# A longer order for the first operations, the values' input on two engines, the attention branch's low parts later, and differences of squares ahead of weights

## The chip, the cores and the metric

The kernel runs on one core of one Trainium2 chip. What counts is the time of one execution on the device, in microseconds (us), as the median of several runs. The engines are named as the profile names them: PE is TensorE (matmuls and transposes), DVE is VectorE, ACT is ScalarE, POOL is GpSimd, and SP issues most transfers. Each has its own queue of instructions, which it works off in order; an instruction waits at the head of its queue until what it reads is there and what it writes is free.

## What is computed

One layer of an encoder on 512 tokens of width 1024, in float32. The input is normalised, one wide projection feeds two branches, neighbourhood attention and a bidirectional Mamba-2 scan (SSD); each is projected back, weighted by a sigmoid gate and summed; then an MLP with squared ReLU follows. Both sub-layers end in a layer norm.

```python
h = layer_norm(x, ln0_g, ln0_b)
proj = u @ w_in          # q | k | v | z | x B C | dt | gates
ya = neighbourhood_attention(q, k, v, rpb) @ w_attn_br
xbc = silu(centred_dwconv(xbc, conv_w, conv_b))
dt = softplus(dt_raw + dt_bias)
y  = ssd_chunked(xs, dt, a, bm, cm) + flipped(...) + xs * d_skip
ys = rms_norm(y * silu(z)) @ w_ssd_br
mix = (sigmoid(gate_a) * ya + sigmoid(gate_s) * ys) @ w_o
h = layer_norm(DN_ALPHA * h + mix, ln1_g, ln1_b)
h = layer_norm(DN_ALPHA * h + square(relu(h @ w_ff1)) @ w_ff2, ln2_g, ln2_b)
```

## The kernel before

**Products in three.** Every large product is made of three matmuls on parts in the float32r format: a number is split into a high part (a cast by ACT) and a low part (the number less its high part, by DVE or POOL), and `mm3` (L359 to L361) adds high by high, low by high and high by low in one PSUM bank. So each slab of weights, 1 MB from memory (`ws_`), becomes `wh_` (ACT) and `wl_` (DVE or POOL) in two halves, one for the input channels 0 to 511 and one for the others, before TensorE can use it. Activations are split in the same way: `hTh` and `hTl`, `yTh` and `yTl`, `aTh` and `aTl`, `sqh` and `sql`.

**Stages.** First the head: the four tiles of 128 tokens `xt0` to `xt3` are loaded, their statistics taken (L501), the inverse root improved by one Newton step (L516 to L520, five small operations), the normalised tiles `xn` written in halves of 512 columns (L526), and transposed by TensorE (`tp_h`, L555). From these ACT makes `hTh` (L562), an engine adds the norm's offset (`hmb`, L568 or L572) and DVE makes `hTl` (L579). This is done for tokens 0 to 255 (first half) and 256 to 511 (second half). The first products are the scan's B and C channels (`wh_bc`, `ps_x`), its step sizes (`ps_dt`, then `dtT` and its transpose `tp_dt`), its x channels (`wh_x`), and its z (`ps_z`). Then come eight groups of the scan, whose results are projected (`ps_sbr`, DVE adds them up in `ysacc`, L1046); the values of the attention (`ps_v`), whose input `hBh` and `hBl` is `hTh` and `hTl` with the tokens in another order (L1125); queries and keys; sixteen heads; the attention's projection (`ps_abr`, L1304 to L1308); the merge and the output projection; the MLP. The MLP's second product (`ff2_strassen`) saves matmuls by Strassen's scheme: its operands are sums and differences of squares (`as_`, L1508) on the left and sums of weights (`w2r`, added up by transfers that accumulate) on the right.

**What sets the order.** Head, scan and their projections are operations of a planner, `Plan`: each has an engine, an estimated duration and the keys that it reads and writes; `Plan.order` simulates the engines with small random changes of the durations (`NUDGES`) and returns an order, in which `issue` emits the operations. Behind the plan the framework's scheduler orders the instructions from the order of the code and their dependencies; `behind(a, b, why)` adds one, so that `a` comes after `b`.

**The last heads.** For each head TensorE makes scores, DVE takes the maximum (L1227), ACT the exponential (L1233), DVE divides by the sum (L1237), TensorE transposes the weights (`tp_p`, two blocks per head), ACT and DVE split them (`pth`, L1252; `ptl`, L1253), and TensorE multiplies with the values (`po`, L1260). `po` has one bank (`yd`), free again when ACT has copied a part of it (`low`, L1271) and DVE has added it into `aT` (L1274). From `aT` ACT makes `aTh`, one k-slice of 128 channels per pair of heads, and DVE `aTl` (L1289); the slices of heads 14 and 15 are k = 7.

## Time and profile before

| | |
|---|---|
| median of 3 runs | 1193.47 us (1192.46 to 1193.9) |
| profiled execution | 1195.13 us, span 1193.4 us |
| PE busy | 1162.2 us (97%) |
| DVE busy | 764.2 us (64%) |
| ACT busy | 606.5 us (51%) |
| POOL busy | 547.3 us (46%) |
| first transpose | 9.88 us |
| last matmul starts | 1184.64 us |

A row of the timeline has the start in us, the duration in us, the engine, the line, the operation, what it writes and reads (partitions times elements), and how often it stands there in a row; in brackets is how long the engine was idle before it and what ended that. In the table of waits, "PE ps_v L359 <- ACT wh_v L341: 1.2, 1, 1.2" is: TensorE, at the matmuls of line 359 that write ps_v, waited 1.2 us in total, once, at most 1.2, and what came last was ACT's wh_v. A 512 wide matmul is followed by the next one after 0.227 us in the dense stretches, though its own row says 0.39, since matmuls overlap. The span is the profiled instructions from first to last; the time of the execution is longer by what lies around it.

### The profile page before, as it was taken

The page shows a single profiled execution, that of the slowest core. Times are in us where ns is not written, and L with a number is a line of the kernel's source. Part 1 is how long each engine was busy: PE and PEld are TensorE (multiplying, and loading weights), DVE is VectorE, ACT ScalarE, POOL GpSimd, SP SyncE. Part 2 cuts the span into 40 slices and gives each one's busy share as a digit, 9 for nine tenths or more (in the row PEclk, how much of TensorE's full clock was granted, in tenths as well). Part 3 has the DMA queues.
Part 4 walks back from the last instruction along what each step waited for, and adds up shares of the span by engine and source line. Part 5 has one row for each costly group of instructions (what it writes and reads, how often), then busy time and mean ns, then how long its engine had stood idle before and what let it go on. Part 6 is the DMA issues. An engine that isn't in the chain of part 4 may idle for free.

```text
span 1193.4 us, 16406 instructions
## 1 busy us (share of the span) xinstructions
PE 1162.2 (97%) x6114; PEld 988.4 (83%) x6114; DVE 764.2 (64%) x1380; ACT 606.5 (51%) x1017; POOL 547.3 (46%) x588
## 2 busy tenths in 40 slices
PE   5999999999999999999999999999999999999997
PEld 5988898989888888788888888888888888878885
DVE  7758375666756666453789975546643567398855
ACT  4586573837354654323667764342353554365510
POOL 1158977787788776403567541016046131221000
PEclk9999999999999999999999999999999999999999
DMA  7144343333333331333333213444336987778511
GB/s 231 57 146 142 89 141 106 107 106 130 106 118 106 124 124 53 106 95 87 92 86 86 59 66 106 143 145 149 95 106 180 239 201 189 183 210 221 162 55 53
DMA packets 129407, 149.19 MB, mean 125 GB/s; under 512 B 22960, under 2 KB 101808, under 8 KB 129328
## 3 DMA queue, kind: packets, MB, share of 16 engines
q1 hardware_dynamic: 115696, 112.63, 30.5%
q0 software_dynamic: 13056, 34.61, 11.9%
q8 instruction: 48, 0.79, 0.3%
q10 hardware_dynamic: 576, 0.92, 0.2%
q14 instruction: 31, 0.25, 0.1%
HBM read 145.90 MB, written 2.23 MB: 124 GB/s over the span
## 4 chain that ended last, share of the span: by engine, by line
PE 83%; DVE 6%; DMA 3%; ACT 3%; issue 3%; POOL 2%; SPq 0%; DVEq 0%; POOLq 0%; ACTq 0%
PE ps_f L361 8%; PE ps_f L359 8%; PE ps_f L360 8%; PE ps_x L361 5%; PE ps_x L359 5%; PE ps_x L360 5%; PE ps_z L359 2%; PE ps_z L360 2%; PE ps_z L361 2%; PE yd L930 2%; DMA w2r<-in_w_ff 2%; PE ps_sbr L361 2%; PE ps_sbr L359 2%; PE ps_sbr L360 2%; PE ps_g L359 2%
## 5 line engine op out<-in xcount | busy, mean ns | idle before, releaser
L737 DVE SCALAR_TENSOR_TENSOR cv<-ps_x,pc,cv 128x511 f32<-128x511 f32 (+1 forms) x128 | 95.8, 748 | 25.3 <-ACT cv L729 21.6
L360 PE MATMUL ps_f<-h1Th,wl_f 128*128 128x512 f32 (+1 forms) x288 | 104.1, 365 | 0.0
L359 PE MATMUL ps_f<-h1Th,wh_f 128*128 128x512 f32 (+1 forms) x288 | 103.7, 366 | 0.0
L361 PE MATMUL ps_f<-h1Tl,wh_f 128*128 128x512 f32 (+1 forms) x288 | 102.0, 365 | 0.0
L1494 DVE TENSOR_TENSOR wl_f<-w2r,wh_f 128x1024 fp32r<-128x1024 f32 x42 | 49.8, 1220 | 63.4 <-ACT wh_f L1493 63.4
L359 PE MATMUL ps_z<-wh_z,hTh 128*128 128x256 f32 x256 | 75.1, 293 | 0.7 <-DVE cv L737 0.7
L361 PE MATMUL ps_z<-wl_z,hTh 128*128 128x256 f32 x256 | 71.4, 279 | 0.0
L360 PE MATMUL ps_z<-wh_z,hTl 128*128 128x256 f32 x256 | 71.3, 279 | 0.0
L1488 POOL DMA_DIRECT2D w2r<-in_w_ff x30 | 36.3, 1416 | 70.7 <-DMA w2r<-in_w_ff 46.5
L359 PE MATMUL ps_f<-wh_f,sqh 128*128 128x512 f32 x168 | 65.3, 391 | 1.3 <-ACT sqh L1493 1.1
L360 PE MATMUL ps_f<-wh_f,sql 128*128 128x512 f32 x168 | 65.3, 390 | 0.2 <-DVE sql L1494 0.2
L361 PE MATMUL ps_f<-wl_f,sqh 128*128 128x512 f32 x168 | 65.3, 390 | 0.2 <-DVE wl_f L1494 0.2
L1493 ACT ACTIVATE wh_f<-w2r 128x1024 fp32r<-128x1024 f32 x42 | 42.6, 1053 | 42.1 <-DMA w2r<-in_w_ff 30.7
L1046 DVE TENSOR_TENSOR ysacc<-ps_sbr,ysacc 128x512 f32<-128x512 f32 x56 | 38.5, 689 | 39.9 <-PE ps_sbr L361 39.7
L359 PEld LDWEIGHTS ps_f<-h1Th,wh_f 128*128 128x128 f32 x288 | 53.9, 188 | 9.0 <-ACT rl L1588 0.3
L360 PEld LDWEIGHTS ps_f<-h1Th,wl_f 128*128 128x128 f32 x288 | 53.9, 188 | 8.8
L342 DVE TENSOR_TENSOR wl_f<-ws_f,wh_f 128x1024 fp32r<-128x1024 f32 x36 | 47.2, 1347 | 20.6 <-ACT wh_f L341 20.5
L361 PEld LDWEIGHTS ps_f<-h1Tl,wh_f 128*128 128x128 f32 x288 | 52.8, 188 | 8.7
L1339 POOL TENSOR_TENSOR gt<-gt,ysacc 128x512 f32<-128x512 f32 x8 | 13.2, 1656 | 100.6 <-ACT gt L1064 92.5
L359 PE MATMUL ps_x<-hTh,wh_bc 128*128 128x512 f32 (+1 forms) x144 | 56.9, 395 | 1.6 <-ACT wh_bc L464 1.6
L359 PE MATMUL ps_sbr<-yTh,wh_sbr 128*128 128x512 f32 x128 | 55.6, 435 | 1.2 <-DVE ysacc L1046 0.6
L360 PE MATMUL ps_x<-hTh,wl_bc 128*128 128x512 f32 (+1 forms) x144 | 53.6, 372 | 1.9 <-POOL wl_bc L467 1.9
(340 smaller groups left out, 3769.1 us busy)
## 6 DMA issues: line engine op xcount, KB each, us to landing
ws_f<-in_w_ff SPq DMA_DIRECT2D x20, 1024.0 KB
w2r<-in_w_ff POOLq DMA_DIRECT2D x18, 1024.0 KB, 7.6
bc<-acs_d SPq DMA_DIRECT2D x32, 512.0 KB
w2r<-in_w_ff POOLq DMA_DIRECT2D x30, 512.0 KB, 9.1
ws_bc<-in_w_in SPq DMA_DIRECT2D x16, 512.0 KB
ws_x<-in_w_in SPq DMA_DIRECT2D x8, 1024.0 KB
ws_z<-in_w_in SPq DMA_DIRECT2D x8, 1024.0 KB
ws_g<-in_w_in SPq DMA_DIRECT2D x8, 1024.0 KB
```

The source lines that it names most:

```text
L342: (eng[i] if isinstance(eng, tuple) else eng).tensor_tensor(out=lo[:, k], in0=st[:, k], in1=hi[:, k].bitcast(F32), op=ALU.subtract)
L359: nc.tensor.matmul(o, lh, rh, start=start, stop=False)
L360: nc.tensor.matmul(o, ll, rh, start=False, stop=False)
L361: return nc.tensor.matmul(o, lh, rl, start=False, stop=stop)
L737: op("DVE", 0.75, lambda j=j, o=o, n=n: nc.vector.scalar_tensor_tensor(out=acc()[:, o], in0=ps()[:, n], scalar=tap(j), in1=acc()[:, o], op ...
L930: nc.tensor.matmul(yd()[:, c % 2, h * HD : (h + 1) * HD], bc()[:, 1, h, :], xtok()[:, c, h * HD : (h + 1) * HD], start=True, stop=True)
L1046: op("DVE", 0.69, lambda d=d, ps=ps: nc.vector.tensor_tensor(out=ysacc[:, d, :], in0=ps(), in1=ysacc[:, d, :], op=ALU.add), r=[(ps.name, 0 ...
L1339: nc.gpsimd.tensor_tensor(out=g1, in0=g1, in1=ysacc[:, d, :], op=ALU.mult)
L1488: nc.gpsimd.dma_start(t, rows(i, n, c, k), accum_op=ALU.add)
L1493: nc.scalar.activation(hi[:, k], x, AF.Copy)
L1494: nc.vector.tensor_tensor(out=lo[:, k], in0=x, in1=hi[:, k].bitcast(F32), op=ALU.subtract)
```

## The change

It has four parts.

1. `HEAD` is a list of the first operations of the plan with the engine that each is to run on (S, D, A, P, T for SP, DVE, ACT, POOL, TensorE); `issue` emits these first, in this order, and then the rest in the order of the planner as before. `ON` takes the engine from the list for the halves of the low weights, `xn`, `hmb` and `wl_dt`. Where one token tile is normalised by itself, two of the Newton step's operations become one, and the operation for an offset that only ACT needs is left out when DVE does both halves.
2. Of the sixteen copies into `hBh` and `hBl`, those of k = 0 to 3 go to ACT, the others stay on DVE. An unused tile, `yT_pad`, is put in front of `yTh`, which moves `yTh` and what lies behind it in the pool's memory.
3. `aTl` for k = 2 to 5 is made behind the last block of the last head's weights. For the first two output blocks of the attention's projection, the high products for k = 0 to 5 are made first, the low ones behind the last head, then k = 6 and 7.
4. Where the left operand of a Strassen product is a difference, the low part of what is split next comes behind the difference.

The first rows of ACT show the head. Before, from the first slab's high part on:

```order
L464 ACTIVATE wh_bc_175<-ws_bc_121 128x1024
L562 ACTIVATE hTh<-tp_h_0_0_157,pc 128x256 x2
L464 ACTIVATE wh_bc_175<-ws_bc_121 128x1024
L568 ACTIVATE hmb_0_192<-hTh,nb_98 128x256
L562 ACTIVATE hTh<-tp_h_0_3_169,pc 128x256
L568 ACTIVATE hmb_6_197<-hTh,nb_98 128x256
L562 ACTIVATE hTh<-tp_h_0_2_166,pc 128x256
```

and with the change, from the first normalised half on:

```order
L572 ACTIVATE xn_147<-xt_113,ln_rs 128x512
L504 ACTIVATE wh_bc_156<-ws_bc_119 128x1024 x2
L606 ACTIVATE hTh<-tp_h_0_0_159,pc 128x256
L613 ACTIVATE hmb_0_186<-hTh,nb_98 128x256
L606 ACTIVATE hTh<-tp_h_0_1_174,pc 128x256
L606 ACTIVATE hTh<-tp_h_0_2_163,pc 128x256
L606 ACTIVATE hTh<-tp_h_0_0_159,pc 128x256
L613 ACTIVATE hmb_2_196<-hTh,nb_98 128x256
L606 ACTIVATE hTh<-tp_h_0_2_163,pc 128x256
L606 ACTIVATE hTh<-tp_h_0_1_174,pc 128x256
```

Both high halves of the slab `wh_bc` stand ahead of the first cast of `hTh`, and an `xn` half ahead of them; the orders of SP and POOL are the same as before in this place.

DVE at the last two heads (`sc` is the softmax of a head, `ptl_0` and `ptl_1` the low parts of the two blocks of its weights). Before, from the sums of head 14 on:

```order
L1235 RECIPROCAL sums_6802<-sums_6802 128x4
L1289 TENSOR_TENSOR aTl_kh<-aT,aTh 128x512 x2
L1289 TENSOR_TENSOR aTl_klz<-aT,aTh 128x512
L1237 TENSOR_SCALAR sc_6800<-sc_6800,sums_6802 128x256 x4
L1289 TENSOR_TENSOR aTl_klz<-aT,aTh 128x512
L1274 TENSOR_TENSOR aT<-po_6598,low_6609 64x8x16 x3
L1274 TENSOR_TENSOR aT<-po_6598,low_6609 64x8x8 x2
L1253 TENSOR_TENSOR ptl_1_6672<-tp_p_1_6666,pth_1_6671 128x512
```

and with the change, from head 15's division on:

```order
L1289 TENSOR_SCALAR sc_6875<-sc_6875,sums_6877 128x256 x4
L1305 TENSOR_TENSOR ptl_0_6831<-tp_p_0_6825,pth_0_6830 128x512
L1327 TENSOR_TENSOR aT<-po_6673,low_6684 64x8x16 x3
L1327 TENSOR_TENSOR aT<-po_6673,low_6684 64x8x8 x2
L1305 TENSOR_TENSOR ptl_1_6840<-tp_p_1_6834,pth_1_6839 128x512
L1342 TENSOR_TENSOR aTl_qs<-aT,aTh 128x512
L1305 TENSOR_TENSOR ptl_0_6908<-tp_p_0_6902,pth_0_6907 128x512
L1327 TENSOR_TENSOR aT<-po_6843,low_6854 64x8x16 x3
L1327 TENSOR_TENSOR aT<-po_6843,low_6854 64x8x8 x2
L1305 TENSOR_TENSOR ptl_1_6917<-tp_p_1_6911,pth_1_6916 128x512
L1342 TENSOR_TENSOR aTl_kh<-aT,aTh 128x512 x2
L1342 TENSOR_TENSOR aTl_klz<-aT,aTh 128x512 x2
```

The four rows of `aTl_kh` and `aTl_klz` stood around head 14's division and now stand behind the last block of head 15.

DVE in the MLP's second product, at the seventh Strassen product's first block (`as_7_0` is the difference, `wl_f_0_7_0` the low weights, `sql` the low squares). Before:

```order
L1494 TENSOR_TENSOR sql_8198<-as_5_1_9361,sqh_8197 128x512
L1494 TENSOR_TENSOR wl_f_0_7_0_9480<-w2r_7_0_9475,wh_f_0_7_0_9479 128x1024 x2
L1508 TENSOR_TENSOR as_7_0_9468<-r_1_8200 128x512 x2
L1494 TENSOR_TENSOR sql_8196<-as_7_0_9468,sqh_8195 128x512 x2
L1508 TENSOR_TENSOR as_7_1_9509<-r_1_8200 128x512 x2
```

and with the change:

```order
L1564 TENSOR_TENSOR sql_8196<-as_5_1_9359,sqh_8195 128x512
L1581 TENSOR_TENSOR as_7_0_9466<-r_1_8198 128x512 x2
L1564 TENSOR_TENSOR wl_f_0_7_0_9478<-w2r_7_0_9473,wh_f_0_7_0_9477 128x1024 x2
L1564 TENSOR_TENSOR sql_8194<-as_7_0_9466,sqh_8193 128x512 x2
L1581 TENSOR_TENSOR as_7_1_9507<-r_1_8198 128x512 x2
```

The difference and the low weights have changed places. The diff, with the list cut:

```diff
-XN_ENG = (("DVE", "DVE"),) * 4
+HEAD = """
+S:xt0.0 S:xt1.0 P:xt2.0 S:pc.0 S:ident.0 S:ws_bc0.1 S:ws_bc0.0 S:xt3.0 S:xt2.0 S:ws_x0.0
+S:ws_dt.0 S:r64.0 S:cst.0 S:msk.0 S:dsk.0 D:st.0.0 D:st.0.1 D:st.1.1 D:mv.0 D:st.1.0
+A:vh.0 D:mv.1 D:nv.1 A:vh.1 D:rs.1 D:xn1.1 A:xn1.0 D:nv.0 D:rs.0 D:xn0.0 A:wh_bc0.0
...
+""".split()
+ON = {x[2:]: x[0] for x in HEAD}
...
         return max(end)
 
     def issue(self):
-        for i in self.order(NUDGES):
+        order = self.order(NUDGES)
+        named = {}
+        for o in self.ops:
+            named.setdefault(".".join(map(str, o["w"][0])), []).append(o["i"])
+        head = [named[x[2:]].pop(0) for x in HEAD]
+        done = set(head)
+        for i in head + [i for i in order if i not in done]:
             self.ops[i]["fn"]()
 
 
...
-        def newton(pr=pr, vh=vh, nv=nv, y=y):
+        def newton(pr=pr, vh=vh, nv=nv, y=y, ts=ts):
             v_.reciprocal(y, vh)
-            v_.tensor_tensor(out=vh, in0=y, in1=y, op=ALU.mult)
-            v_.tensor_tensor(out=vh, in0=vh, in1=nv, op=ALU.mult)
+            if len(ts) == 1:
+                v_.scalar_tensor_tensor(out=vh, in0=y, scalar=y, in1=nv, op0=ALU.mult, op1=ALU.mult)
+            else:
+                v_.tensor_tensor(out=vh, in0=y, in1=y, op=ALU.mult)
+                v_.tensor_tensor(out=vh, in0=vh, in1=nv, op=ALU.mult)
             v_.scalar_tensor_tensor(out=y, in0=vh, scalar=1.5, in1=y, op0=ALU.add, op1=ALU.mult)
-            v_.scalar_tensor_tensor(out=rs[:, pr, 1], in0=mv[:, pr, 0], scalar=-1.0, in1=y,
-                                    op0=ALU.mult, op1=ALU.mult)
+            if any(ON[f"xn{t}.{j}"] == "A" for t in ts for j in range(2)):
+                v_.scalar_tensor_tensor(out=rs[:, pr, 1], in0=mv[:, pr, 0], scalar=-1.0, in1=y,
+                                        op0=ALU.mult, op1=ALU.mult)
...
             op("ACT", 0.5, lambda c=c: nc.scalar.activation(yz()[:, c, :], yz()[:, c, :], AF.Copy,
                                                             scale=rt["y"]()[:, c : c + 1]),
                r=[(rt["y"].name, 0), (yz.name, c)], w=[(yz.name, c)])
-        yTh = local(f"yTh{g}", "yTh", [P, 2, S], F32R)
+        def make():
+
+            if g == 0:
+                sbp.tile([P, 1728], F32, name="yT_pad")
+            return sbp.tile([P, 2, S], F32R, tag="yTh", bufs=1, name=f"yTh{g}")
+
+        yTh = Plan.Tile(plan, f"yTh{g}", "yTh", make)
         yTl = local(f"yTl{g}", "yTl", [P, 2, S], F32R)
         for i in range(2):
             tpy = bank(f"tp_y{g}_{i}", "tr", [P, NT, P])
...
     blk = "p (r b j) -> p b r j"
     for k in range(KD):
         for src, dst in ((hTh, hBh), (hTl, hBl)):
-            nc.vector.tensor_copy(dst[:, k, :].rearrange("p (b r j) -> p b r j", r=8, b=4),
-                                  src[:, k, :].bitcast(F32).rearrange(blk, r=8, b=4))
+            d4 = dst[:, k, :].rearrange("p (b r j) -> p b r j", r=8, b=4)
+            s4 = src[:, k, :].bitcast(F32).rearrange(blk, r=8, b=4)
+            if k < 4:
+                nc.scalar.activation(d4, s4, AF.Copy)
+            else:
+                nc.vector.tensor_copy(d4, s4)
     for s in range(2):
         pss = [psx.tile([P, 512], F32, tag=tag, bufs=BANKS[tag], name=f"ps_v{s}_{b}")
                for b, tag in enumerate(("so", "tr", "so", "tr"))]
...
                 pth = atp.tile([P, 2, 2, P], F32R, tag="pth", bufs=3, name=f"pth{h}_{b2}")
                 ptl = atp.tile([P, 2, 2, P], F32R, tag="ptl", bufs=3, name=f"ptl{h}_{b2}")
                 nc.scalar.activation(pth, tp, AF.Copy)
-                nc.vector.tensor_tensor(out=ptl, in0=tp, in1=pth.bitcast(F32), op=ALU.subtract)
+                spread = nc.vector.tensor_tensor(out=ptl, in0=tp, in1=pth.bitcast(F32),
+                                                 op=ALU.subtract)
                 pts.append((pth, ptl))
             po = psx.tile([P, 4, P], F32, tag="yd", bufs=BANKS["yd"], name=f"po{h}")
 
...
         t = atp.tile([P, n, S], F32R, tag=tag, name=f"aTl_{tag}")
         aTl.extend(t[:, i] for i in range(n))
     for k in range(KD):
-        nc.vector.tensor_tensor(out=aTl[k], in0=aT[:, k], in1=aTh[:, k].bitcast(F32),
-                                op=ALU.subtract)
+        low = nc.vector.tensor_tensor(out=aTl[k], in0=aT[:, k], in1=aTh[:, k].bitcast(F32),
+                                      op=ALU.subtract)
+        if 2 <= k < 6:
+            behind(low, spread, "the last head's weights")
 
 
     ya = app.tile([P, KD, S], F32, tag="aT", name="ya")
...
         wa = weights([(w_attn_br, 0, d2 * 256, 256)], KD, 256, f"abr{d2}",
                      nc.vector if d2 else nc.gpsimd,
                      after=(ins.ins, ins.ins) if d2 == 1 else None)
+        tag = ("so", "mm")[d2 % 2]
+        pss = [psx.tile([P, S], F32, tag=tag, bufs=BANKS[tag], name=f"ps_abr{2 * d2 + j}")
+               for j in range(2)]
+
+        def steps(j, ks, parts):
+            ins = []
+            for k in ks:
+                w = [t[:, k, j * P : (j + 1) * P] for t in wa]
+                for p, (u, v) in enumerate(((w[0], aTh[:, k, :]), (w[1], aTh[:, k, :]), (w[0], aTl[k]))):
+                    if p in parts:
+                        ins.append(nc.tensor.matmul(pss[j], u, v, start=k + p == 0,
+                                                    stop=k == KD - 1 and p == 2))
+            return ins
+
+        if d2:
+            for j in range(2):
+                steps(j, range(KD), (0, 1, 2))
+        else:
+
+            for j in range(2):
+                steps(j, range(6), (0, 1))
+            for j in range(2):
+                behind(steps(j, range(6), (2,))[0], last, "the last head")
+            for j in range(2):
+                steps(j, range(6, KD), (0, 1, 2))
         for j in range(2):
-            d = 2 * d2 + j
-            tag = ("so", "mm")[d2 % 2]
-            ps = psx.tile([P, S], F32, tag=tag, bufs=BANKS[tag], name=f"ps_abr{d}")
-            for k in range(KD):
-                w = [t[:, k, j * P : (j + 1) * P] for t in wa]
-                first = nc.tensor.matmul(ps, w[0], aTh[:, k, :], start=k == 0, stop=False)
-                if (d, k) in ((0, 6), (1, 0)):
-                    behind(first, last, "the last head")
-                nc.tensor.matmul(ps, w[1], aTh[:, k, :], start=False, stop=False)
-                nc.tensor.matmul(ps, w[0], aTl[k], start=False, stop=k == KD - 1)
-            nc.scalar.activation(ya[:, d, :], ps, AF.Copy)
+            nc.scalar.activation(ya[:, 2 * d2 + j, :], pss[j], AF.Copy)
     at.__exit__(None, None, None)
     vpool.__exit__(None, None, None)
 
...
 
 
         np_ = len(r2)
-        begun, made, fetched = set(), [0], [0]
+        begun, made, fetched, first = set(), [0], [0], []
 
         def rows(i, n, c, k=slice(0, 4)):
             r0 = q0 * D + (i * np_ + c) * 512
...
         def split(hi, lo, src):
             for x, k in zip(src, halves):
                 nc.scalar.activation(hi[:, k], x, AF.Copy)
-                nc.vector.tensor_tensor(out=lo[:, k], in0=x, in1=hi[:, k].bitcast(F32),
-                                        op=ALU.subtract)
+                low = nc.vector.tensor_tensor(out=lo[:, k], in0=x, in1=hi[:, k].bitcast(F32),
+                                              op=ALU.subtract)
+                if first:
+                    behind(low, first[-1], "the difference of squares first")
+            first.clear()
             return hi, lo
 
         def left(name, c, x, y=None):
...
             if y is not None:
                 t = ffp.tile([P, 4, 256], F32, tag="asum", bufs=1, name=f"as_{h}_{name}_{c}")
                 for i, k in enumerate(halves):
-                    nc.vector.tensor_tensor(out=t[:, k], in0=src[i], in1=part(*y, k), op=ALU.subtract)
+                    diff = nc.vector.tensor_tensor(out=t[:, k], in0=src[i], in1=part(*y, k),
+                                                   op=ALU.subtract)
                 src = [t[:, k] for k in halves]
             pair = pairs[made[0] % len(pairs)]
             made[0] += 1
-            return split(*pair, src)
+            both = split(*pair, src)
+            if y is not None:
+                first.append(diff)
+            return both
 
         def right(name, c, x):
             return split(*parts(f"f2_{h}_{name}_{c}", [P, 4, 512]), x)
```

71 lines of the change are left out of this document (48 added, 23 removed).

## The prediction

> **What bounds the kernel now.** I read the page's busy times first, then the table of waits of TensorE, then the timeline of each place named there.
>
> ```profile
> PE 1162.2 (97%) x6114; PEld 988.4 (83%) x6114; DVE 764.2 (64%) x1380; ACT 606.5 (51%) x1017; POOL 547.3 (46%) x588
> PE tp_h L555 <- DVE xn L526: 9.9, 1, 9.9
> PE po L1260 <- DVE aT L1274: 2.0, 2, 1.4
> PE ps_x L360 <- POOL wl_bc L467: 1.9, 1, 1.9
> PE ps_x L359 <- ACT wh_bc L464: 1.6, 1, 1.6
> PE ps_v L359 <- ACT wh_v L341: 1.2, 1, 1.2
> PE ps_f L359 <- ACT sqh L1493: 1.1, 1, 1.1
> ```
>
> TensorE is busy for 97% of the 1193.4 us. The change takes away no matmul, so it can only shorten the 31 us in which TensorE is idle, and the time in which it runs slowly. Of those 31 us, 9.9 lie ahead of the first transpose. The next five rows, 7.8 us, are the four places that the change touches. An idle engine elsewhere is no gain. Of what stands in a queue only what TensorE waits for counts, and time won there stays won only if every later wait of TensorE moves with it.
>
> **1. The head.** These are the rows of TensorE and of the engines that feed it, in the first 36 us.
>
> ```profile
> 10.15 1.06 ACT L464 ACTIVATE wh_bc<-ws_bc 128x1024 fp32r<-128x1024 f32 x1 [2.33 <-DMA ws_bc<-in_w_in]
> 11.24 1.23 DVE L467 TENSOR_TENSOR wl_bc<-ws_bc,wh_bc 128x1024 fp32r<-128x1024 f32 x1
> 14.08 1.05 ACT L464 ACTIVATE wh_bc<-ws_bc 128x1024 fp32r<-128x1024 f32 x1
> 14.67 0.68 DVE L501 BATCH_NORM_STATS2 ln_st<-xt 128x6 f32<-128x512 f32 x1
> 15.22 2.35 POOL L467 TENSOR_TENSOR wl_bc<-ws_bc,wh_bc 128x1024 fp32r<-128x1024 f32 x1 [10.50 <-ACT wh_bc L464]
> 17.62 0.58 PE L360 MATMUL ps_x<-hTh,wl_bc 128*128 128x256 f32 x1 [1.86 <-POOL wl_bc L467]
> 22.22 0.41 PE L359 MATMUL ps_x<-hTh,wh_bc 128*128 128x256 f32 x1
> 22.44 0.40 PE L360 MATMUL ps_x<-hTh,wl_bc 128*128 128x256 f32 x1
> 22.65 0.30 PE L361 MATMUL ps_x<-hTl,wh_bc 128*128 128x256 f32 x1
> 22.79 0.28 PE L359 MATMUL ps_x<-hTh,wh_bc 128*128 128x256 f32 x1
> 35.42 0.28 PE L361 MATMUL ps_dt<-hTl,wh_dt 128*64 128x256 f32 x1
> 35.74 0.59 ACT L629 ACTIVATE dtT<-ps_dt 64x512 f32<-64x512 f32 x1 [2.81 <-PE ps_dt L361]
> 51.10 0.28 PE L359 MATMUL ps_z<-wh_z,hTh 128*128 128x256 f32 x1
> ```
>
> TensorE works in one piece from 17.62, when GpSimd ends the second low half of the first slab. GpSimd began that only at 15.22, because ScalarE made the high half behind two casts of hTh, at 14.08. After the change ScalarE makes both high halves back to back, from 10.15 to 10.15 + 2 x 1.05 = 12.25, and GpSimd is done at 12.25 + 2.35 = 14.6. VectorE is then the later one: the low half at 11.24 to 12.47, three statistics at 0.64 to 0.68 each, now ahead of the first hTl (14.4), and that hTl of 0.48: 14.9. So the piece begins at 14.9 in place of 17.62: 2.7 us.
>
> TensorE needs one k-slice per three to nine matmuls of 0.21 us each at the low pitch; ScalarE (a cast of hTh and, for half of them, one of hmb) and VectorE some 1.0 us per slice, so neither starves it. The 19 pitches from 17.62 to 22.65 take 5.03 us, where 19 at 0.213 (two of them lie between 22.22 and 22.65) take 4.05: 1.0 us went in small waits. With the second products of each slice filled in between I count 0.7 of it as won. From 21 us the new order gives ScalarE 9 us of work in one piece, ending near 30.2; the last hTl follows at 30.8 and the last ps_dt near 31.5, by TensorE's own work 35.70 - 2.7 - 0.7 - 0.3 = 32.0 (three x matmuls of 0.113 now come behind it). TensorE still bounds. Cover: if ScalarE's piece were 1 us longer, it would cost 0.5.
>
> The pitch halves at 22.65, 5.03 us after the start of the piece. I let it halve 5 us after the new start, near 19.9. If it stays at 22.65, a matmul that would have taken 0.113 takes 0.213 for those 2.75 us, and 1.3 us of the gain are lost. Sum of the head: **-3.4 us**, to the first ps_z (51.10, then 47.7), from -1.5 (clock late, half of the small waits back) to -4.4 (all of them gone).
>
> [...]
>
> **2. The values' input.**
>
> ```profile
> 495.34 2.00 ACT L341 ACTIVATE wh_v<-ws_v 128x1024 fp32r<-128x1024 f32 x2
> 506.18 0.39 PE L361 MATMUL ps_sbr<-yTl,wh_sbr 128*128 128x512 f32 x1
> 506.61 0.69 DVE L1046 TENSOR_TENSOR ysacc<-ps_sbr,ysacc 128x512 f32<-128x512 f32 x1 [0.67 <-PE ps_sbr L361]
> 506.66 2.01 ACT L341 ACTIVATE wh_v<-ws_v 128x1024 fp32r<-128x1024 f32 x2 [9.31 <-issue]
> 507.22 0.42 DVE L1125 CAST hBh<-hTh 128x512 fp32r<-128x512 f32 x1
> 507.78 1.17 PE L359 MATMUL ps_v<-wh_v,hBh 128*128 128x512 f32 x4 [1.21 <-ACT wh_v L341]
> ```
>
> The wait is put down to wh_v, but that had been done since 495.34 + 2.00 = 497.34; TensorE really waits for the first hBh, which stands behind the last ysacc, itself waiting for the last ps_sbr. The pitch is 0.227, so 507.78 - 506.18 - 0.23 = 1.37 us are lost. Eight copies move to ScalarE, which was idle for 9.31 us here: at 0.6 each (its 64x512 op at 718.59 below takes 0.59) they end near 502, and the unused tile ahead of yTh keeps them from waiting for yTh's memory. What they delay on ScalarE, the second wh_v, begins at 506.66 anyway. VectorE's eight end 2.7 us sooner. **-1.3 us**; from 0 (the copies wait for the last ps_sbr after all) to -1.5.
>
> **3. The branch's low parts.**
>
> ```profile
> 701.16 1.68 DVE L1289 TENSOR_TENSOR aTl_kh<-aT,aTh 128x512 fp32r<-128x512 f32 x2
> 713.52 0.36 PE L1260 MATMUL po<-pth,vhl 128*128 128x256 f32 x1 [0.65 <-DVE aT L1274]
> 715.89 0.94 DVE L1274 TENSOR_TENSOR aT<-po,low 64x128 f32<-64x128 f32 x5 [0.52 <-ACT low L1271]
> 716.98 0.36 PE L1260 MATMUL po<-pth,vhl 128*128 128x256 f32 x1 [1.35 <-DVE aT L1274]
> 718.59 0.59 ACT L1271 ACTIVATE low<-po 64x512 f32<-64x512 f32 x1 [2.11 <-PE po L1261]
> 723.27 3.21 DVE L342 TENSOR_TENSOR wl_abr<-ws_abr,wh_abr 128x1024 fp32r<-128x1024 f32 x2 [0.17 <-ACT wh_abr L341]
> ```
>
> Beyond the normal pitch, po of heads 14 and 15 start 0.8 and 1.6 us late, together 2.4: each waits for VectorE to empty the one yd bank. VectorE loses four low parts (1.68 for two of them) ahead of the last softmax and does them behind ptl15_1, so head 15's softmax runs some 2.8 us sooner; nine matmuls of the branch (2.0 us) stand ahead of po15, which covers low14 (0.6) and the adds (0.94). Both stalls should go. But six more branch matmuls (1.4 us) now precede po15, so po15 ends only 2.4 - 1.4 = 1.0 us sooner, and the chain behind it (low, the sigmoid's table, gt, aTh7, wh_abr1, wl_abr1) moves by 1.0 while TensorE wants wl_abr1 2.4 us sooner. Before, its first half was ready at 723.27 + 3.21 / 2 = 724.9, and TensorE came for it near 725.5, 0.6 later; so 2.4 - 1.0 - 0.6 = 0.8 is late again. **-1.6 us**; from -0.8 (the aTl and aTh7 chain late too) to -2.4.
>
> **4. Differences of squares.**
>
> ```profile
> 1044.10 1.06 ACT L1493 ACTIVATE wh_f<-w2r 128x1024 fp32r<-128x1024 f32 x1 [5.05 <-DMA w2r<-in_w_ff]
> 1046.29 0.39 PE L361 MATMUL ps_f<-h1Tl,wh_f 128*128 128x512 f32 x1
> 1046.33 1.29 DVE L1508 TENSOR_TENSOR as<-r 128x512 f32<-128x512 f32 x2
> 1047.05 1.29 ACT L1493 ACTIVATE sqh<-as 128x512 fp32r<-128x512 f32 x2 [1.90 <-DVE as L1508]
> 1047.73 0.50 PE L359 MATMUL ps_f<-wh_f,sqh 128*128 128x512 f32 x1 [1.06 <-ACT sqh L1493]
> 1048.46 0.50 PE L360 MATMUL ps_f<-wh_f,sql 128*128 128x512 f32 x1 [0.23 <-DVE sql L1494]
> ```
>
> The differences need nothing that is still on its way, yet stand behind a weight half that waits for a transfer. Ahead of it they are done long before; ScalarE casts sqh right behind wh_f, 1045.16 to 1046.45, and VectorE's first sql, now behind the weight half that ScalarE released at 1045.16, ends near 1047.1. TensorE's stall of 1047.73 - 1046.29 - 0.23 = 1.21 goes, and that for sql (0.50) shrinks a little. **-1.3 us**; from 0 (w2r lands that much later) to -1.9.
>
> **Sum.** -3.4 - 1.3 - 1.6 - 1.3 = -7.6. The profiled execution took 1195.13 us, 1.7 around its span; it lies 1.7 above the median of 1193.47. I predict a span of about 1185.8 and a median of **1185.9 us**, on its own 1183.5 to 1188.5.
>
> **Rivals.**
> A. *The head gives half.* ScalarE gets the xn, hTh, hmb and weight casts in one piece, and VectorE can be held up by GpSimd:
>
> ```profile
> 20.92 2.39 POOL L467 TENSOR_TENSOR wl_x<-ws_x,wh_x 128x1024 fp32r<-128x1024 f32 x1 [3.35 <-ACT wh_x L464]
> 22.10 1.24 DVE L511 TENSOR_SCALAR ln_v<-ln_mv 128x2 f32<-128x2 f32 x1
> ```
>
> A two-element op took 1.24 us until GpSimd's slab half ended at 23.31. In the new order that slab half lies near 28.2 to 30.6, beside the last hmb and hTl; two such blocks, or x tiles that land after VectorE reaches their statistics (14.67 is when they were read, not when they landed), cost some 2.4: 1188.3. Against it: GpSimd's first half ends at 14.6 in the new order, before the first hTl.
> B. *The last two places hand theirs on*: wl_abr1 late by all it can be and w2r pacing TensorE: -0.8 and 0 in place of -1.6 and -1.3: 1188.0.
> C. *Slower: the clock stays low.* If the piece at 14.9 is broken often enough that the pitch stays at 0.21 through the second transposes, each us after 19.9 costs half of one. It outweighs the whole sum from 19.9 + 15.2 = 35.1 on; up to the first ps_z, near 47.7, it costs 13.9: 1199.8. For it: the transposes from 9.9 on did not bring the short pitch, which came 13 us later. Against it: the new queue holds 45 matmuls, 9.6 us at the low clock, ahead of the next transpose, and small waits of up to 0.6 us did not prevent it before. [...]
> D. *No change*: the w2r stream, not TensorE, sets the last stage, and what came before is waited away at 1044. For it, the 5.05 us that ScalarE waited for w2r; against it, the stream's transfers start when TensorE's results free their buffers, so they move too. Only the tail would count: about 1192.
>
> **How the numbers follow.** Forecast 0.56, A 0.16, B 0.11, C 0.05, D 0.07; 0.05 for more than forecast (all stalls gone, 1182). The range takes the forecast's own, A, B and the better case down to 1181.8 and up to 1190.5, leaving out C and most of D. Within 0.2% means within 2.4 us, which is what a measurement here can tell from no change: faster 0.56 + 0.16 + 0.11 + 0.05 = 0.88, same 0.07, slower 0.05.
>
> **What would show it.** Right: the matmul that waited at 17.62 near 15, the pitch halved near 20, dtT near 32, ps_z from 47.7; ps_v right behind ps_sbr; no wait of po for aT and a new one, under 1 us, of ps_abr for wl_abr; no wait of ps_f for sqh. Wrong: dtT later than 34, hB copies on ScalarE beginning only after the last ps_sbr, a wait for wl_abr over 1.6, or a shift at 900 us that is gone at 1060.

## The result and the profile after

The changed kernel takes 1186.38 us (median of 6 runs, 1185.48 to 1187.55), the kernel before 1193.93 us beside it (6 runs). The ratio is 0.9936, with a 95% interval from 0.9924 to 0.9949: 7.5 us faster, where 7.6 had been predicted (1185.9 us). The profiled execution took 1186.48 us, its span is 1184.7 us.

The page's busy row and four rows of TensorE's table of waits, for the changed kernel:

```profile
PE 1158.4 (98%) x6114; PEld 988.1 (83%) x6114; DVE 757.0 (64%) x1361; ACT 614.7 (52%) x1033; POOL 546.6 (46%) x588
...
PE tp_h L599 <- DVE xn L575: 10.2, 1, 10.2
PE ps_x L401 <- DVE hTl L621: 1.8, 1, 1.8
...
PE ps_abr L1363 <- DVE wl_abr L382: 0.9, 1, 0.9
...
PE ps_f L400 <- DVE sql L1564: 0.3, 1, 0.3
```

The rows of before for po, ps_v and ps_f behind sqh are gone, the two for ps_x have become one, and ps_abr is new. TensorE has as many matmuls as before. Its busy time is 3.8 us lower and the span 8.7, so more than half of the gain is idle time that went.

The four places in the changed kernel's timeline. First the head:

```profile
9.96 2.01 ACT L504 ACTIVATE wh_bc<-ws_bc 128x1024 fp32r<-128x1024 f32 x2 [0.62 <-DMA ws_bc<-in_w_in]
10.17 3.27 PE L599 MATMUL tp_h<-cst,xn 128*128 128x128 f32 x16 [10.17 <-DVE xn L575]
12.06 2.44 POOL L508 TENSOR_TENSOR wl_bc<-ws_bc,wh_bc 128x1024 fp32r<-128x1024 f32 x1 [7.48 <-ACT wh_bc L504]
12.20 1.87 DVE L542 BATCH_NORM_STATS2 ln_st<-xt 128x6 f32<-128x512 f32 x3
13.49 1.47 ACT L606 ACTIVATE hTh<-tp_h,pc 128x256 fp32r<-128x256 f32 x3 [0.52 <-PE tp_h L599]
14.99 0.48 DVE L621 SCALAR_TENSOR_TENSOR hTl<-tp_h,pc,hmb 128x256 fp32r<-128x256 f32 x1 [0.93 <-ACT hTh L606]
15.53 0.39 PE L401 MATMUL ps_x<-hTl,wh_bc 128*128 128x256 f32 x1 [1.85 <-DVE hTl L621]
31.86 0.59 ACT L671 ACTIVATE dtT<-ps_dt 64x512 f32<-64x512 f32 x1 [1.38 <-PE ps_dt L401]
47.34 0.28 PE L399 MATMUL ps_z<-wh_z,hTh 128*128 128x256 f32 x1
```

ScalarE makes both high halves in one go, GpSimd ends its low half at 14.50, and the dense work begins at 15.53 in place of 17.62. The first ps_z comes at 47.34, 3.76 us earlier. Then the values and the branch:

```profile
494.05 0.61 ACT L1176 ACTIVATE hBh<-hTh 128x512 fp32r<-128x512 f32 x1
503.00 0.39 PE L401 MATMUL ps_sbr<-yTl,wh_sbr 128*128 128x512 f32 x1
503.22 1.07 PE L399 MATMUL ps_v<-wh_v,hBh 128*128 128x512 f32 x4
707.02 0.37 PE L1313 MATMUL po<-pth,vhl 128*128 128x256 f32 x1
710.73 0.28 PE L1313 MATMUL po<-pth,vhl 128*128 128x256 f32 x1
712.09 0.59 ACT L1324 ACTIVATE low<-po 64x512 f32<-64x512 f32 x1 [2.40 <-PE po L1314]
714.76 3.00 POOL L1409 TENSOR_TENSOR gt<-gt,ysacc 128x512 f32<-128x512 f32 x2 [17.02 <-ACT gt L1112]
716.76 3.21 DVE L382 TENSOR_TENSOR wl_abr<-ws_abr,wh_abr 128x1024 fp32r<-128x1024 f32 x2 [0.16 <-ACT wh_abr L381]
718.89 0.50 PE L1363 MATMUL ps_abr<-aTh,wl_abr 128*128 128x512 f32 x1 [0.89 <-DVE wl_abr L382]
```

ps_v stands one pitch (0.22 us) behind the last ps_sbr, since ScalarE had begun its copies 9 us earlier. Both last output products come without a wait (no bracket), and the weights' low half is now late by 0.89 us. Last, the squares:

```profile
1036.89 1.06 ACT L1563 ACTIVATE wh_f<-w2r 128x1024 fp32r<-128x1024 f32 x1 [5.01 <-DMA w2r<-in_w_ff]
1037.86 1.14 ACT L1563 ACTIVATE sqh<-as 128x512 fp32r<-128x512 f32 x2
1039.18 0.39 PE L399 MATMUL ps_f<-wh_f,sqh 128*128 128x512 f32 x1
1039.87 0.50 PE L400 MATMUL ps_f<-wh_f,sql 128*128 128x512 f32 x1 [0.30 <-DVE sql L1564]
```

sqh follows wh_f directly, where ScalarE had stood idle for 1.90 us, and TensorE no longer waits for it.

### The profile page after: what moved, and what is told of

Its sections match the earlier page's. It is cut to its first block, busy times and chain, and to the rows that moved or that the text cites. A ratio compares the mean times of both kernels' runs of the same rounds, so it can differ in the third digit from the quotient of the medians.

```text
span 1184.7 us, 16407 instructions
## 1 busy us (share of the span) xinstructions
PE 1158.4 (98%) x6114; PEld 988.1 (83%) x6114; DVE 757.0 (64%) x1361; ACT 614.7 (52%) x1033; POOL 546.6 (46%) x588
## 4 chain that ended last, share of the span: by engine, by line
PE 90%; DVE 3%; DMA 3%; issue 1%; ACT 1%; POOL 1%; DVEq 0%; SPq 0%; POOLq 0%; ACTq 0%
PE ps_f L399 8%; PE ps_f L401 8%; PE ps_f L400 8%; PE ps_x L401 5%; PE ps_x L399 5%; PE ps_x L400 5%; PE ps_abr L1363 3%; PE ps_g L399 2%; PE ps_g L401 2%; PE ps_g L400 2%; PE ps_z L399 2%; PE ps_sbr L399 2%; PE ps_z L400 2%; PE ps_z L401 2%; PE ps_sbr L401 2%; PE yd L972 2%
## 5 line engine op out<-in xcount | busy, mean ns | idle before, releaser
L401 PE MATMUL ps_x<-hTl,wh_bc 128*128 128x512 f32 (+1 forms) x144 | 53.6, 372 | 1.8 <-DVE hTl L621 1.8
```

Of the source, the lines that this page charges most:

```text
L401: return nc.tensor.matmul(o, lh, rl, start=False, stop=stop)
```

## The experiments

Since each edit of the change moves TensorE at one place, the traces can be laid over each other: the n-th matmul of one against the n-th of the other. The step at a place is by how much that difference changes from just ahead of it to just behind it. It compares two single executions, so whatever only one of them met at that place stands in it too. The four parts were run one at a time first.

**Part 1 alone** (`HEAD`, `ON` and what reads them, put into the kernel before).

```diff
+HEAD = """
+S:xt0.0 S:xt1.0 P:xt2.0 S:pc.0 ...
+""".split()
+        for i in head + [i for i in order if i not in done]:
```

> Part 1 of the change alone, the rest as before. Theory (four separate stalls, each worth what its own place gives, no part needs another): tp_dt starts near 32.8 in place of 36.66, first ps_z near 47.3 in place of 51.10, and the shift stays: ps_v 3.2 us sooner than before, the end 3.2 to 3.6 us sooner; time 1190.3 to 1190.8 where before is 1193.9. Rival (the last stage is paced by the w2r transfers): the shift is there at 700 us but not at 1060 us, time within 1.5 us of before. Rival (the head is worth little and the others more): tp_dt moves by under 2 us.

**Part 2 alone.**

```diff
+            if g == 0:
+                sbp.tile([P, 1728], F32, name="yT_pad")
...
+            if k < 4:
+                nc.scalar.activation(d4, s4, AF.Copy)
+            else:
+                nc.vector.tensor_copy(d4, s4)
```

> Part 2 alone: eight copies on ScalarE and the unused tile. Theory: nothing moves ahead of 500 us; the wait of ps_v (1.21 us) is gone, everything behind is 1.4 to 1.5 us sooner, time 1192.4. Rival (the copies wait for the memory of yTh, or the eight copies hold up ScalarE's next weights): the wait of ps_v remains in part, time within 0.7 us of before.

**Part 3 alone.**

```diff
+        if 2 <= k < 6:
+            behind(low, spread, "the last head's weights")
...
+            for j in range(2):
+                steps(j, range(6), (0, 1))
+            for j in range(2):
+                behind(steps(j, range(6), (2,))[0], last, "the last head")
```

> Part 3 alone: low parts late and the branch's products reordered. Theory: both waits of po for aT are gone (2.4 us), a wait of 0.8 to 0.9 us of ps_abr for wl_abr is new; the matmuls behind 730 us are 1.6 to 2.0 us sooner, time 1191.9 to 1192.3. Rival (the new wait eats it all): shift under 0.8 us.

**Part 4 alone.**

```diff
+                if first:
+                    behind(low, first[-1], "the difference of squares first")
...
+            if y is not None:
+                first.append(diff)
```

> Part 4 alone: the difference of squares ahead of the low weights. Theory (the wait comes from VectorE's order, not from the transfer): the wait of ps_f for sqh (1.06 us) is gone; with the smaller waits around it 1.3 to 1.9 us from 1060 us on, time 1192.0 to 1192.6. Rival (part 4 only pays when TensorE comes 6.7 us sooner, as with the whole change): under 0.7 us.

The four, each timed beside the kernel before (1194.7 us, 33 runs), and TensorE's steps against the profile of before, in us. The last column is a second profile of the changed kernel (`after_again`, below).

| | part 1 | part 2 | part 3 | part 4 | all | all, again |
|---|---|---|---|---|---|---|
| median, us | 1191.97 | 1193.74 | 1191.77 | 1193.16 | 1186.38 | 1187.18 |
| ratio to before | 0.9978 | 0.9996 | 0.9978 | 0.9989 | 0.9936 | 0.9931 |
| 95% interval | 0.9969 to 0.9987 | 0.9987 to 1.0005 | 0.9966 to 0.9989 | 0.9979 to 1.0 | 0.9924 to 0.9949 | 0.9917 to 0.9945 |
| step, start to first tp_dt | -3.61 | -0.37 | -0.36 | -0.27 | -3.88 | -3.72 |
| step at the first ps_v | 0.00 | -1.46 | 0.00 | 0.00 | -1.47 | -1.47 |
| step over the last heads and ps_abr | +0.05 | +0.04 | -1.96 | +0.01 | -2.00 | -1.93 |
| step at the squares | -1.80 | -1.90 | -1.85 | -2.97 | -1.93 | -2.99 |

The second and third rows of steps are clean: each part acts at its own place, whether the others are there or not, and with its full size. The first row needs a correction: parts 2, 3 and 4 leave the head as it was, and yet it ends 0.27 to 0.37 us earlier in them, so the profile of before was late there by about 0.3, and part 1 is worth some 3.3 us at this place. By the ratios the parts are worth 2.6, 0.5, 2.6 and 1.3 us, together 7.0 of the 7.6 that the whole ratio gives, so they add up within the intervals.

Against what had been expected: parts 2 and 3 did in their traces what their theories say. Part 2's time does not show it, since its interval reaches from 1.6 us faster to 0.6 slower. Part 1 missed: its first ps_v came 2.76 us sooner than before, not 3.2, because 0.7 of the gain at the first ps_z was lost on the way, and its time fell by 2.6 us, not by 3.1 to 3.6. Part 4's time is at the lower end of its theory, but its step at the squares has to be read with the next paragraph.

The fourth row is not clean: the kernels *without* part 4 gained 1.8 to 1.9 us at the squares too. That much of the stall belonged to the one execution that was profiled before. ScalarE's cast wh_f and TensorE's product behind it, in the timeline of part 1 alone, whose squares are as before:

```profile
1039.68 1.06 ACT L1535 ACTIVATE wh_f<-w2r 128x1024 fp32r<-128x1024 f32 x1 [4.94 <-DMA w2r<-in_w_ff]
1042.63 1.29 ACT L1535 ACTIVATE sqh<-as 128x512 fp32r<-128x512 f32 x2 [1.89 <-DVE as L1550]
1043.32 0.49 PE L399 MATMUL ps_f<-wh_f,sqh 128*128 128x512 f32 x1
1044.04 0.50 PE L400 MATMUL ps_f<-wh_f,sql 128*128 128x512 f32 x1 [0.23 <-DVE sql L1536]
```

Here the transfer of w2r let wh_f begin 3.6 us ahead of TensorE's product (1043.32 - 1039.68), and sqh came just in time, although the differences still stand behind a weight half. In the profile of before, w2r came so late that only 2.4 us lay between wh_f (1044.10) and the moment TensorE was ready (1046.29 + 0.23), and sqh was 1.21 late. Its late w2r had also stopped TensorE once before, 26 us ahead of that:

```profile
1020.86 1.06 ACT L1493 ACTIVATE wh_f<-w2r 128x1024 fp32r<-128x1024 f32 x1 [6.18 <-DMA w2r<-in_w_ff]
1021.98 0.50 PE L359 MATMUL ps_f<-wh_f,sqh 128*128 128x512 f32 x1 [0.21 <-ACT wh_f L1493]
```

This product waits for the cast of w2r itself, not for a difference of squares. With two longer pitches behind it the place cost 0.6 us, and in no other profile, with part 4 or without, does it cost anything.

**The changed kernel once more.**

> The changed kernel once more, for a second profile of it beside the variants. Its time should be 1186 to 1187 again. Theory (the place of the squares differs from profile to profile by when the transfer of the second layer's weights lands, 6.4 to 8.7 us after ScalarE asks for it): TensorE's place behind the squares' first column differs from the first profile of the changed kernel by 0.5 us or more against its place ahead of it, most likely 0.7 to 1.1 us earlier. Rival (each kernel has its own stall there): the same step to within 0.2 us.

Measured: 1187.18 us (5 runs, 1184.88 to 1187.37), and a step at the squares 1.06 us larger than in the first profile, as the theory said. The same rows in this second profile:

```profile
1037.81 1.06 ACT L1563 ACTIVATE wh_f<-w2r 128x1024 fp32r<-128x1024 f32 x1 [4.62 <-DMA w2r<-in_w_ff]
1038.77 1.14 ACT L1563 ACTIVATE sqh<-as 128x512 fp32r<-128x512 f32 x2
1041.09 0.39 PE L399 MATMUL ps_f<-wh_f,sqh 128*128 128x512 f32 x1
1041.32 0.39 PE L400 MATMUL ps_f<-wh_f,sql 128*128 128x512 f32 x1
```

wh_f stands 3.28 us ahead of TensorE (in the first profile 1039.18 - 1036.89 = 2.29), and nothing waits. The pitches of over 0.3 us at this place, where 0.227 is normal, cost TensorE in all, without part 4: 2.9 (before, with the 0.6 at 1022), 1.2, 1.0 and 1.1 us (parts 1, 2, 3 alone); with part 4: 0.9 (first profile of the changed kernel), and between 0.0 and 0.6 in its second profile, part 4 alone and the variants below, in six of these nine nothing. So part 4 is worth about 1.1 us where w2r is early and 1.3 (2.26 less 0.94) where it is late. This second profile also has a wait that no part touches, of yo for t, 1.3 us, at 357.6 us: single profiles wander by such amounts.

**Without the unused tile.**

```diff
-            if g == 0:
-                sbp.tile([P, 1728], F32, name="yT_pad")
```

> The changed kernel without the tile yT_pad, so that the eight values' copies of ScalarE land again on addresses that the last attention products still read. Theory (the tile is what lets the copies start at 494 us in the changed kernel): the first copy hBh now waits for the last ps_sbr, near 503 us, the eight copies end near 508 us, and ps_v waits at least 1 us behind ps_sbr again; TensorE's place behind the branch's start is 1 to 5 us later than in the changed kernel, time 1187.5 to 1191. Rival (VectorE's four copies moved to ScalarE are the whole of it, the address is free long before): ps_v still follows ps_sbr at once, time as the changed kernel's, about 1186.4.

Measured: 1185.68 us (0.9926, 0.9912 to 0.994), no worse than with it. In its timeline the address does to seven copies what it was said to do, and not to the first:

```profile
493.26 0.62 ACT L1174 ACTIVATE hBh<-hTh 128x512 fp32r<-128x512 f32 x1
502.63 0.63 ACT L1174 ACTIVATE hBl<-hTl 128x512 fp32r<-128x512 f32 x1 [8.75 <-PE ps_sbr L401]
...
502.21 0.39 PE L401 MATMUL ps_sbr<-yTl,wh_sbr 128*128 128x512 f32 x1
502.43 1.07 PE L399 MATMUL ps_v<-wh_v,hBh 128*128 128x512 f32 x4
503.34 0.47 PE L400 MATMUL ps_v<-wh_v,hBl 128*128 128x512 f32 x1
```

Seven of ScalarE's eight copies wait 8.75 us for the last ps_sbr. But the first does not, and it is all that ps_v needs to begin: four products on hBh take 0.91 us, by when the first hBl is there (502.63 + 0.63 = 503.26 against 503.34), and nothing behind it waits. The theory was right on seven copies and wrong on the first, near 503 us by it and at 493.26 in the trace, which is the one that TensorE waits for: the tile is worth nothing that shows. What part 2 wins it wins by the second engine, by which the first copy no longer stands behind the last ysacc.

**The low parts early again**, with the new order of the products kept.

```diff
-        if 2 <= k < 6:
-            behind(low, spread, "the last head's weights")
```

> The changed kernel without the call that moves the branch's low parts behind others: the low parts 2 to 5 stand again where the kernel before had them, ahead of the last head's softmax work on VectorE, with the new order of the gate products kept. Theory (the low parts stand in front of the last head's work, and this is where the branch's stall came from): the wait of head 14's output product, 0.7 to 0.9 us, comes back, VectorE's division for head 15 is 1 to 2 us later than in the changed kernel, time 1187.0 to 1188.4. Rival (the order of the products alone did the work): no wait of 0.5 us or more at the last two heads' output products and the time of the changed kernel, about 1186.4.

Measured: 1188.03 us (0.9946, 0.9932 to 0.9959), in the range of the theory. TensorE's two waits of this place:

```profile
712.54 0.36 PE L1313 MATMUL po<-pth,vhl 128*128 128x256 f32 x1 [1.35 <-DVE aT L1327]
720.97 0.50 PE L1361 MATMUL ps_abr<-aTh,wl_abr 128*128 128x512 f32 x1 [0.88 <-DVE wl_abr L382]
```

The wait of the last head's product is back with the 1.35 us that it had before (head 14's, which I had named, is not), the wait for wl_abr stays, and the step over the place is 2.07 us worse than in the changed kernel, which is all of part 3. The order of the products alone is worth nothing; without the dependency of the low parts nothing of part 3 is left. The dependency with the old order of the products was not run.

**The last gates early.**

```diff
-                nc.scalar.activation(pth, tp, AF.Copy)
+                cast = nc.scalar.activation(pth, tp, AF.Copy)
...
-    gates.append([merge_gates(1, 0, ("cb", "mm")), merge_gates(1, 1, ("mm", "cb"), last)])
+    gates.append([merge_gates(1, 0, ("cb", "mm")), merge_gates(1, 1, ("mm", "cb"), cast)])
```

> The changed kernel with the last gates' sigmoid, and the table load ahead of it, put on ScalarE before the low part of the last head rather than behind it. ScalarE stands idle for 2.40 us there in the changed kernel, and table load and two sigmoids take 2.55 us. Theory (the chain low part, table load, sigmoids, aTh, wh_abr, wl_abr sets the first gate product, which waited 0.89 us): low part at most 0.2 us later, the weights' cast about 1 us or more earlier, the wait of ps_abr for wl_abr gone, time 0.7 to 1.0 us under the changed kernel's, about 1185.5. Rival (another operand, the last head's aT, sets that start as well): the wait keeps its length under another name, time about 1186.4.

Measured: 1186.54 us (0.9936, 0.9924 to 0.9948): the rival's time, and a wait of the old length under another name, though for aTl_klz and not for the last head's aT. The table load (1.28 us, from 711.98) went into ScalarE's idle time as intended, and yet:

```profile
714.03 3.04 POOL L1409 TENSOR_TENSOR gt<-gt,ysacc 128x512 f32<-128x512 f32 x2 [14.03 <-ACT gt L1112]
...
712.94 1.29 DVE L1342 TENSOR_TENSOR aTl_kh<-aT,aTh 128x512 fp32r<-128x512 f32 x2
714.15 3.48 DVE L1342 TENSOR_TENSOR aTl_klz<-aT,aTh 128x512 fp32r<-128x512 f32 x2
720.29 2.36 DVE L382 TENSOR_TENSOR wl_abr<-ws_abr,wh_abr 128x1024 fp32r<-128x1024 f32 x2 [0.26 <-ACT wh_abr L381]
...
717.68 0.73 PE L1363 MATMUL ps_abr<-aTl_klz,wh_abr 128*128 128x512 f32 x2 [0.96 <-DVE aTl_klz L1342]
```

The gates released GpSimd's products 3.0 us earlier (714.03, less the 2.26 us by which this whole profile is later, against 714.76), so these now run beside two other low parts of VectorE, which took 3.48 us where the two of the same form just ahead took 1.29. The weights' low part, no longer beside GpSimd, took 2.36 where it takes 3.21 in the changed kernel. So there was a third theory: what TensorE waits for at this place is GpSimd's work beside VectorE's.

**GpSimd's products late.**

```diff
+            lows[name] = (eng[i] if isinstance(eng, tuple) else eng).tensor_tensor(
...
-            nc.gpsimd.tensor_tensor(out=g1, in0=g1, in1=ysacc[:, d, :], op=ALU.mult)
+            g = nc.gpsimd.tensor_tensor(out=g1, in0=g1, in1=ysacc[:, d, :], op=ALU.mult)
+            if d2 == 1:
+                behind(g, lows["abr1"], "the next weights' low part")
```

> The changed kernel with GpSimd's two products of the second gates (gt times ysacc, 3.0 us in all) put behind the low part of the branch's second weights on VectorE. In the changed kernel they run from 714.8 to 717.8 us, beside that low part. Theory (VectorE's two halves of wl_abr take 3.21 us rather than 2.36 us because GpSimd works at the same time, and TensorE's wait of 0.89 us for wl_abr is that): the pair takes 2.3 to 2.5 us, the wait falls under 0.2 us, time 0.7 to 0.9 us under the changed kernel's. Rival (the halves wait for ScalarE's wh_abr, GpSimd does not matter): pair 3.0 us or more or the wait 0.7 us or more, time the changed kernel's.

Measured: 1184.44 us (0.9918, 0.9904 to 0.9933), 2.7 us under the changed kernel of the same job (1187.18), though the two intervals overlap. Of that the trace gives this place 0.84 us; the rest is other places and runs.

```profile
716.20 2.36 DVE L384 TENSOR_TENSOR wl_abr<-ws_abr,wh_abr 128x1024 fp32r<-128x1024 f32 x2 [0.25 <-ACT wh_abr L383]
718.64 3.38 POOL L1411 TENSOR_TENSOR gt<-gt,ysacc 128x512 f32<-128x512 f32 x2 [21.45 <-DVE wl_abr L384]
```

The pair takes 2.36 us, GpSimd begins when it is done, and ps_abr's wait has left the table of waits. That is the theory, in each of its numbers but the time, which fell by more.

**Early gates and late products together.**

```diff
+    gates.append([merge_gates(1, 0, ("cb", "mm")), merge_gates(1, 1, ("mm", "cb"), cast)])
...
+            if d2 == 1:
+                behind(g, lows["abr1"], "the next weights' low part")
```

> The early gates together with GpSimd's late products. With the early gates alone VectorE's low parts of the last heads took 3.48 us for two rather than 1.29 us, beside GpSimd's products, and the wait of 0.89 us only changed its name. Theory (GpSimd beside VectorE is what ate the early gates): the two low parts take 1.3 us again, ScalarE's last aTh is 0.5 us or more earlier than in the changed kernel against TensorE's place, no wait over 0.2 us at ps_abr, time 0.7 to 1.0 us under the changed kernel's, that is as with the late products alone. Rival (the early gates delay the last head's low part on ScalarE as well): a wait of 0.5 us or more stays at ps_abr.

Measured: 1186.04 us, but with runs from 1183.69 to 1188.58 (0.9931, 0.9913 to 0.9949), so the time tells nothing. The trace does: the low parts take 1.29 us for two again, ScalarE's last aTh comes 0.9 us earlier, nothing waits at ps_abr, and the step over the place is 1.18 us under the changed kernel's, 0.33 more than with the late products alone. GpSimd beside VectorE was what ate the early gates.

**Another head order.**

```diff
-...T:tp_h0_0_1.0 A:hTh.0.0 T:tp_h0_0_3.0 D:st.3.1 T:tp_h0_0_2.0 P:wl_bc0.1
-S:ws_bc1.1 A:hmb0_0.0 T:tp_h0_0_1.1 D:st.3.0 A:hTh.2.0 D:st.2.1 A:hTh.5.0 A:hTh.1.0
+...T:tp_h0_0_1.0 A:hTh.0.0 A:hTh.1.0 T:tp_h0_0_3.0 D:st.3.1 T:tp_h0_0_2.0 P:wl_bc0.1
+S:ws_bc1.1 A:hmb0_0.0 T:tp_h0_0_1.1 D:hmb0_1.0 D:hTl.1.0 D:hTl.0.0 A:hTh.2.0 A:hTh.3.0 D:st.3.0
...
```

> The changed kernel with another order of its first operations: the second transposed block's high part right behind the first's, and both low parts ahead of the later statistics. Theory (the first dense product waits 1.85 us for a low part that VectorE could make 1 us earlier): dense work starts near 14.4 us rather than 15.5, and the head's end, the transposes of dt, comes 0.3 to 1.3 us earlier than 32.78 us, time 1185.1 to 1186.1. Rival (the later blocks' supply sets the head's end: the last low part was ready 0.8 us before TensorE took it, and the two casts of weights come when they come): the early start is lost again in waits for hTl or x's statistics between 16 and 31 us, dt's transposes within 0.3 us of 32.78, time about 1186.4.

Measured: 1185.6 us (0.9934, 0.992 to 0.9947). Both theories get a part.

```profile
12.88 1.74 DVE L616 TENSOR_SCALAR hmb<-hTh,pc 128x256 f32<-128x256 f32 x1
15.66 0.39 PE L401 MATMUL ps_x<-hTl,wh_bc 128*128 128x256 f32 x1 [1.31 <-DVE hTl L621]
18.90 0.33 PE L400 MATMUL ps_dt<-hTh,wl_dt 128*64 128x256 f32 x1 [0.41 <-DVE wl_dt L585]
32.37 0.46 PE L676 MATMUL tp_dt<-cst,dtT 64*128 64x64 f32 x4
```

The start did not move (15.66): an offset of VectorE that takes 0.35 us alone took 1.74 us beside GpSimd's half of the slab, which ended at 14.46. This order did not get past that; no run moved the half slab to show that it is the cause here. dt's transposes come 0.40 us earlier all the same, which is less than the 0.7 us by which they differ among the eight profiles with the head order of the change (last section). The first ps_dt came at 18.21 for 19.39, since the clock stayed full there (1.00 between 16 and 20 us, for 0.58 and 0.57; last section); 0.8 of these 1.2 us went again, 0.41 of it in the new wait for wl_dt.

**Head order and late products together.**

```diff
+S:ws_bc1.1 A:hmb0_0.0 T:tp_h0_0_1.1 D:hmb0_1.0 D:hTl.1.0 D:hTl.0.0 A:hTh.2.0 A:hTh.3.0 D:st.3.0
...
+            if d2 == 1:
+                behind(g, lows["abr1"], "the next weights' low part")
```

> The two that may add up: the other head order (dt's transposes 0.4 us earlier) and GpSimd's late products (0.7 to 0.9 us). Theory: 1.1 to 1.3 us under the changed kernel of the same job, near 1185.2. Rival (either is given back at the next wait): within 0.5 us of the changed kernel.

Measured: 1184.13 us (4 runs, 1183.74 to 1185.47; 0.9914, 0.99 to 0.9928). It is the fastest of all, 3.0 us under the changed kernel of the same job, whose runs reach from 1184.88 to 1187.37. The trace confirms 0.22 us of it in the head and 0.82 at the branch; against the late products alone (1184.44) it is not told apart.

## Why the prediction was right

**The sum.** -7.6 was predicted and -7.5 measured. Its four terms were -3.4, -1.3, -1.6, -1.3; the steps were -3.9 (-3.8 at the first ps_z, -3.4 there against parts 2 to 4 alone), -1.5, -2.0 and, for part 4 itself, -1.1 to -1.3. That the sum came out within 0.1 us is luck: the interval of the ratio alone is 3 us wide, and 0.6 to 2.4 us of the shift were lost between the first ps_z and the first ps_v in the two profiles of the changed kernel. The profiled spans differ by 8.7 us, more than the times do, because the profile of before had a late w2r and lay 1.7 above the median, as the prediction had noted for its own time without asking where in the span it lay.

**The head.** Right in its end (dtT at 31.86 for 32.0, ps_z at 47.34 for 47.7), wrong in two steps on the way. First, "14.9, VectorE is then the later one": the piece began at 15.53, and what came last was not VectorE's statistics, done at 14.07, but the last of ScalarE's three casts of hTh, at 13.49 + 1.47 = 14.96. In the new order the cast for the second block stands behind those for the later ones, and the first low part waits for it (0.93 us in the row at 14.99). Why it waits for a cast of another block stays open; the two blocks share one bank of PSUM, and no run tried them in separate banks. Second, "I let it halve 5 us after the new start": the long pitch did not go by the length of the piece. It was gone when the piece began, came back for 3.4 us, and went again at 19.73, near the 19.9 of the forecast, by luck. The late start of 0.6 us was in part given back by the short pitch: the six pitches up to 16.44 took 0.91 us, where six of 0.213 take 1.28. The 0.4 us over the term, at the first ps_z, are about what the profile of before was late: parts 2, 3 and 4 alone reach their first ps_z 0.27 to 0.37 us ahead of it with the old head. Against these three the changed kernel gains 3.4 us, the term itself.

**The values.** Mechanism and size held: -1.46 or -1.47 in each of three traces, against -1.3 and a lower end of -1.5. The sentence on the unused tile, and the sign "hB copies on ScalarE beginning only after the last ps_sbr", named a real effect and gave it the whole term's weight: without the tile seven copies begin that late, and it costs nothing that shows.

**The branch.** Both waits went and the new one came, at 0.89 us for the 0.8 worked out. The term is 0.4 too small because it counted only the waits that the table names: the output products of the last three heads themselves ran with longer pitches before, 3.85 us for their 27 pitches where they take 3.07 in the changed kernel. That is 0.8; the rest of it went into the new wait, which costs 1.15 us in pitches and not 0.8. The chain given for the rest (low, table, gates, aTh, weights) was the place but not the cause: with the table out of the chain the wait stayed, with GpSimd out of VectorE's way it was gone. The 3.21 us in the row that the prediction quoted were already the price of that; 2.36 is the price without.

**The squares.** The mechanism held, in the profile that it was read from: "TensorE's stall of 1.21 goes", and the wait for sql stayed near its 0.5, as the first profile of the changed kernel shows. Both profiles have a late w2r, and between them part 4 is worth 1.3 us, as forecast. But that was the price for a late w2r. In the three traces of parts 1 to 3 alone, which have the old order, there is no wait for sqh that the table names; what goes then are the waits for sql and for the next weight half, 1.1 us, which the term let only "shrink a little". So the term held for the case that it was read from, and for the other the size came out near it by luck, from waits that it had not counted. Part 4 alone was timed at -1.3 us (0 to -2.5). The lower end, "w2r lands that much later", was the right doubt.

**The rivals.** A (the head gives half) did not come about, but its mechanism, VectorE held up by GpSimd, is what caused the branch's last wait and, by the row, stopped the other head order. B did not: the shift is 6.7 us ahead of the squares and grows behind them. C did not: the short pitch was there in the head's first product. D is refuted by the same shift: the w2r stream moved with TensorE, and its cast at the squares began at 1036.89 for 1044.10.

## What to carry to other kernels

A wait in one profile that follows a transfer's landing is one draw: before it becomes a term, look for the same wait in a second profile of the kernel, or bound it by how far ahead of its reader the landing was. When VectorE's operation takes longer than its form does elsewhere in the trace, look at what GpSimd does in the same microseconds; moving that work, off the critical path by itself, was worth 0.84 us here, nearly as much as part 4. When engines share a stage, run the parts singly: steps of TensorE over a place told them apart to 0.1 us where the times told them apart to 1 us. It is also worth comparing the profile of before with kernels that leave a place as it was: what they gain there does not belong to the change.
